# Quarter sums of two feed-forward stages moved from GpSimd to VectorE, and modulation steps placed later, in a whole diffusion-model forward pass on one core

## The chip, the core and the metric

The program runs on one core of a Trainium2 chip. A core has a matrix engine (TensorE, PE in the profile; its weight loads are PEld), three engines for elementwise work (VectorE is DVE, ScalarE is ACT, GpSimd is POOL), and SyncE (SP), whose queue issues the DMA transfers. Each engine runs its own instructions strictly in the order in which they stand, and waits at an instruction until what it needs is there. The metric is the device time of one execution, in microseconds (us); lower is better.

## The reference, cut to what matters

Two transformer-like blocks (512 tokens of `x`, 256 of `ctx`, width 1024) are computed in float32. Between attention and state-space mixers stand four gated feed-forward layers, and scales, shifts and gates come from a "modulation" product:

```python
def swiglu(h, w_in, w_out):
    gate, up = jnp.split(h @ w_in, 2, axis=-1)          # w_in 1024 x 5632, w_out 2816 x 1024
    return (jax.nn.silu(gate) * up) @ w_out
...
mod_x = jax.nn.silu(c) @ mod_w[layer] + mod_b[layer]     # six vectors of 1024; the second block has nine
mod_c = jax.nn.silu(c_ctx) @ mod_w[layer] + mod_b[layer]
shm_x, scm_x, gm_x, shf_x, scf_x, gf_x = ...
x = layer_norm(ALPHA * x + gf_x * swiglu(x * (1.0 + scf_x) + shf_x, ffn_w_in[layer], ffn_w_out[layer]), ...)
```

## The kernel before

**Float32 from two halves.** TensorE is fed with a rounded half `hi` and a remainder `lo` of every float32 operand, and three products stand for one. `split` (lines 64 and 65) makes the halves: ACT casts `whi`, then DVE subtracts to get `wlo`. Weights come in by DMA as `raw` or `sr`, 512 KB at a time.

**Two feed-forward layers in quarters.** The first and the third feed-forward layer have 768 tokens; `first_product_quarters` computes their `h @ w_in` with seven products of quarter matrices instead of eight. A step `j` (22 of them) is one block of 128 gate columns and the same 128 up columns. For `j` = 0 and 1 (`LEAD`) it works plainly, in four calls of `whole`, because the sums of the activations are not there yet; each `whole` ends in a product `lg` of ACT and DVE (lines 524 and 525) that frees its PSUM bank, and all four share one `lg` buffer. From `j` = 2 on, seven products of 12 matmuls each run per step, and their operands are sums of quarters: `h.sums` forms those of the activations once (tiles `ts`, lines 428 to 431, halved into `tq`), and `load` and `weight` form those of the weights for every `j`: four sums of 128x512 (`sx` and `sr`, line 502), 80 per layer, all on POOL. Two of the activation sums are on POOL too (lines 429 and 431, three times each). Evacuations of the step's PSUM banks are DVE's `c` (570, 579, 585) and `g` (582, 587). After the last `whole` the fourth quarter of the activations is overwritten with its sum (`fourth`, which issues casts `hhi` and subtractions `hlo`).

**Modulation between the matmuls.** Modulation vectors needed later are worked out in small steps on a list `c.fill`: for one vector there are eight `part` steps (a 512 KB load `graw` and a DVE multiply-add into `acc`, lines 228 and 230, one for `x` and often one for `ctx`), a `finish` (adds the bias, line 236, sums over partitions with matmuls of line 244, writes the row to DRAM), and a `turn` (reads the row back as `fmrow` and transposes it on PE, line 257). `c.run_fill(n)` issues the next `n` steps. In the two layers in quarters one step is run in each `whole`, after each `j` and after each group of the second product.

**The order of the work.** A scheduler places the instructions of each engine once, when the program is built; `high_priority` moves a part ahead (`WPRIO`, 400 places) or, with a negative offset, back. Weight loads, casts and sums have `WPRIO`, the multiply-adds have -150. At run time every engine keeps that order.

Of the kernel before, what the change touches and what calls it, by code (L numbers as in the profile page):

```python
# [389 lines left out]
class Quarters:  # L390
# [26 lines left out]

    def sums(self, pool):

        c, nc = self.c, self.c.nc  # L420
        rest = []
        for i in range(self.half):
            f1, f2 = (pool.tile([P, KT, P], F32, tag=f"f{j}", name=c.nm("f"), bufs=2) for j in range(2))
            nc.sync.dma_start(f1, self.fd[i])
            nc.sync.dma_start(f2, self.fd[i + self.half])
            s = pool.tile([P, 3, 4, P], F32, tag="ts", name=c.nm("ts"), bufs=1)
            s4 = pool.tile([P, 4, P], F32, tag="ts4", name=c.nm("ts4"), bufs=self.half)
            nc.vector.tensor_tensor(s[:, 0], f2[:, :4], f1[:, :4], ALU.subtract)
            nc.gpsimd.tensor_tensor(out=s[:, 2], in0=f2[:, 4:], in1=f2[:, :4], op=ALU.subtract)
            nc.vector.tensor_tensor(s[:, 1], f2[:, 4:], s[:, 0], ALU.subtract)  # L430
            nc.gpsimd.tensor_tensor(out=s4, in0=f1[:, 4:], in1=s[:, 1], op=ALU.subtract)
            o = slice(i * P, (i + 1) * P)
            c.split(s, self.t[0][:, :, :, o], self.t[1][:, :, :, o])
            rest.append((s4, o))

        def fourth():
            for s4, o in rest:
                c.split(s4, self.hi[:, 2, :, o], self.lo[:, 2, :, o])

        return fourth  # L440
# [37 lines left out]
def first_product_quarters(c, h, T, w_in, gd, nfill, pool):  # L478
# [22 lines left out]
    def sums(o, x, y, op):  # L501
        nc.gpsimd.tensor_tensor(out=o, in0=x, in1=y, op=op)

    def load(j):
        with c.tc.high_priority(offset=WPRIO):
            r = []
            for b, o in enumerate((0, FFN_H)):
                x = pool.tile([P, KT, P], F32, tag=f"sr{b}", name=c.nm("sr"), bufs=3 - b)
                nc.sync.dma_start(x, w_in[:, o + j * P : o + (j + 1) * P].rearrange("(k p) n -> p k n", p=P))
                r += [x[:, :4], x[:, 4:]]  # L510
            r.append(pool.tile([P, 4, P], F32, tag="sx", name=c.nm("sx"), bufs=2))
            raw[j] = r
            sums(r[4], r[0], r[2], ALU.subtract)
            sums(r[2], r[2], r[3], ALU.add)

    with c.tc.tile_pool(name=c.nm("fs"), bufs=1) as fp:
        ws = [[c.wcols(w_in, o + j * P) for o in (0, FFN_H)] for j in range(LEAD)]

        def whole(j, v, outs):
# [6 lines left out]
            nc.sync.dma_start(gd[j][:, v * n : v * n + n], g)  # L526
            c.run_fill(nfill)

        for j in range(LEAD):
            whole(j, 0, (one(j), two(j)))  # L530
        fourth = h.sums(fp)
        for j in range(LEAD, LEAD + 2):
            load(j)
        for j in range(LEAD):
            whole(j, 1, (c.ps("px")[:, :n], c.ps("px")[:, :n]) if j % 2 == 0 else (one(0), two(0)))
        fourth()

# [6 lines left out]
    with c.tc.tile_pool(name=c.nm("fm"), bufs=1) as mp:  # L544
        W, S, X = {}, {}, {}

        def weight(j, i, hi, lo):

            if j not in raw:
                load(j)  # L550
            r = raw[j]
            c.split(r[{1: 0, 2: 1, 3: 1, 4: 3, 5: 2, 6: 0, 7: 4}[i]], hi, lo)
            if i == 1:
                sums(r[0], r[3], r[4], ALU.subtract)
            elif i == 2:
                sums(r[1], r[1], r[0], ALU.subtract)
            W[j, i] = hi, lo

        def run(j, i):
# [23 lines left out]
            elif i == 3:  # L583
# [4 lines left out]
                nc.sync.dma_start(gd[j], g)  # L588
                c.run_fill(nfill)

        for s in range(0, len(order), 2):
            with c.tc.high_priority(offset=WPRIO):
                hi = c.whl.tile([P, 2, 4, P], F32R, tag="hi", name=c.nm("whi"))
# [582 lines left out]
def main(c, I, out, stop=None):  # L1176
# [6 lines left out]
    modp = [None]  # L1183

    def accs(pool):
        return lambda: pool.tile([P, D], F32, tag="acc", name=c.nm("acc"))
# [91 lines left out]
    with tc.tile_pool(name="mix0", bufs=1) as mp:  # L1278
        mix = mp.tile([P, 6, D], F32, name="mix")
        og, od = mix[:, :, :512], mix[:, :, 512:]  # L1280
        with tc.tile_pool(name="dif", bufs=1) as dp:
# [10 lines left out]
            with tc.tile_pool(name="gla", bufs=1) as gp:  # L1292
# [4 lines left out]
                modp[0] = lambda: df.pair()[:, :D]  # L1297
                c.fill += block1(0, 2, "gm0", "row") + block1(0, 4, "scf0", "fm") + block1(0, 3, "shf0", "fm")
                c.run_fill(3)
# [54 lines left out]
    with tc.tile_pool(name="modp1", bufs=2) as mq:  # L1354
        modp[0] = accs(mq)
        c.fill += block1(0, 5, "gf0", "row") + block1(1, 1, "scm1", "fm") + block1(1, 0, "shm1", "fm")
        c.fill += block1(1, 2, "gm1", "row", False) + block1(1, 4, "scf1", "fm", False)
        c.fill += block1(1, 3, "shf1", "fm", False)
        ln = LnTail(c, None, I, 0, 1, 6, {v: f"gf0{v}" for v in "xc"}, xdt(0),
                    ln_sc("01", 0, 1, "scm1", "shm1", "xc"), xd[1], "xc" if stop else "x", 768,  # L1360
                    out=out if stop == "ln2" else None)
        ffn(c, h, 768, I["ffn_w_in"][0], I["ffn_w_out"][0], ln, (1, 1))
        h = ln.h
# [31 lines left out]
    with tc.tile_pool(name="modp2", bufs=2) as mq:  # L1395
        modp[0] = accs(mq)
        c.fill += block1(1, 5, "gf1", "row", False) + block2(0, "fm") + block2(1, "fm") + block2(2, "row")
        ln = LnTail(c, None, I, 1, 1, 4, {"x": "gf1x"}, xdt(2), lambda: ada_sc(0, 0, "xc"), xd[3], "x", 768,
# [18 lines left out]
    with tc.tile_pool(name="modp3", bufs=2) as mq:  # L1417
        modp[0] = accs(mq)
        c.fill += block2(3, "fm") + block2(4, "fm") + block2(5, "row", False) + block2(6, "fm", False)
        c.fill += block2(7, "fm", False) + block2(8, "row", False)  # L1420
        ad = AdaTail(c, None, 6, lambda pool: ada_gate(pool, 0, 2, 0.5, "xc"),
                     lambda t: xdt(3)(t) if t < 4 else ctx2(t), lambda: ada_sc(1, 3, "xc"), xd[0], 768,
                     out if stop == "f1" else None)
        ffn(c, h, 768, I["ffn1_w_in_2"][0], I["ffn1_w_out_2"][0], ad, (1, 1))
        h = ad.h
# [744 lines left out]
```

## Time and profile before

| | |
|---|---|
| Runs without the profiler | 3641.51, 3643.37, 3630.83 us (median 3641.51) |
| Profiled execution | 3632.67 us, of which the span of the trace is 3630.9 us |
| Busy share of the span | PE 94%, PEld 80%, DVE 65%, ACT 45%, POOL 18% |
| Mean granted clock of PE | 0.974 of full speed |
| DMA | 522.53 MB, mean 144 GB/s |

The first layer in quarters begins its first product at about 543 us and ends it at about 905 us; the third layer does so from about 2110 to 2451 us. In both, POOL is busy 33 to 43% of the time.

### The profile page before, as it was taken

What the parts mean: (1) busy time and instruction counts of PE and PEld (TensorE: products, weight loads), DVE (VectorE), ACT (ScalarE), POOL (GpSimd) and SP (SyncE); (2) the same over time, 40 slices, a digit from 0 to 9 for tenths busy, and PEclk for the clock granted to TensorE, in tenths of its full rate; (3) what the DMA queues carried; (4) which work ended last, traced back from release to release, by engine and by line L of the source; (5) the groups of instructions that cost most, each with busy time, mean ns of one, the idle gap of its engine ahead of it and who ended that gap; (6) DMA issues with size and microseconds to landing.
All of it is one profiled execution on the core that took longest, in us unless ns stands there. A gap on an engine that the chain in (4) does not pass through costs nothing.

```text
span 3630.9 us, 48754 instructions
## 1 busy us (share of the span) xinstructions
PE 3412.6 (94%) x18316; PEld 2903.6 (80%) x18316; DVE 2372.8 (65%) x3578; ACT 1641.7 (45%) x2719; POOL 649.9 (18%) x481
## 2 busy tenths in 40 slices
PE   8999987999989999988999979999999999999998
PEld 5877776999778877767887769998787798878887
DVE  6766667676687577766566786766766585663235
ACT  5335533444345555533334634343556454553234
POOL 0001124433020354443000133430000000000000
PEclk9999998999999999989999989999999999999999
DMA  6330135443774333344666753436751122354356
GB/s 226 111 88 27 47 116 181 134 125 102 244 249 149 87 101 103 101 157 160 219 196 203 261 189 104 134 114 221 252 183 40 52 63 73 108 180 151 119 169 217
DMA packets 446834, 522.53 MB, mean 144 GB/s; under 512 B 21272, under 2 KB 357268, under 8 KB 446597
## 3 DMA queue, kind: packets, MB, share of 16 engines
q1 hardware_dynamic: 446597, 519.41, 45.0%
q8 instruction: 144, 2.36, 0.3%
q14 instruction: 93, 0.76, 0.1%
HBM read 452.49 MB, written 62.64 MB: 142 GB/s over the span
## 4 chain that ended last, share of the span: by engine, by line
PE 34%; issue 9%; DVE 4%; DMA 4%; ACT 2%; POOL 1%; SPq 0%; DVEq 0%; POOLq 0%; ACTq 0%
PE big L99 7%; PE big L113 5%; PE px L113 5%; PE px L496 4%; PE px L99 4%; PE big L496 3%; DMA gr<-gd 1%; DVE wlo L65 1%; PE mm L1606 1%; PE mm L1779 1%; PE big L1571 1%; ACT whi L64 1%; PE mm L1600 1%; PE big L1569 0%; DVE acc L230 0%
## 5 line engine op out<-in xcount | busy, mean ns | idle before, releaser
L65 DVE TENSOR_TENSOR wlo<-raw,whi 128x1024 fp32r<-128x1024 f32 (+1 forms) x444 | 542.3, 1226 | 476.3 <-ACT whi L64 440.9
L64 ACT CAST whi<-raw 128x1024 fp32r<-128x1024 f32 (+1 forms) x444 | 457.7, 1033 | 673.7 <-PE big L99 216.4
L99 PE MATMUL big<-hhi,whi 128*128 128x512 f32 (+1 forms) x1312 | 444.9, 364 | 10.0 <-ACT hhi L64 5.8
L99 PE MATMUL big<-hlo,whi 128*128 128x512 f32 (+1 forms) x1312 | 437.6, 359 | 5.3 <-DVE hlo L65 5.3
L99 PE MATMUL big<-hhi,wlo 128*128 128x512 f32 (+1 forms) x1312 | 439.4, 360 | 0.0
L133 POOL TENSOR_TENSOR s<-s,mhalf 128x1 f32<-128x1 f32 (+1 forms) x106 | 76.3, 721 | 1989.0 <-DVE s L131 1976.0
L99 PEld LDWEIGHTS big<-hhi,whi 128*128 128x128 f32 x1312 | 237.6, 192 | 55.1 <-issue 7.8
L99 PEld LDWEIGHTS big<-hlo,whi 128*128 128x128 f32 x1312 | 236.4, 191 | 42.9 <-DVE hlo L65 6.6
L99 PEld LDWEIGHTS big<-hhi,wlo 128*128 128x128 f32 x1312 | 236.3, 191 | 37.2 <-issue 1.9
L230 DVE SCALAR_TENSOR_TENSOR acc<-graw,silu_c,acc 128x1024 f32<-128x1024 f32 x168 | 223.9, 1355 | 33.5 <-DMA graw<-in_mod_w_dram 16.4
L65 DVE TENSOR_TENSOR wlo<-sr,whi 128x512 fp32r<-128x512 f32 x240 | 187.0, 813 | 60.6 <-ACT whi L64 59.9
L64 ACT CAST whi<-sr 128x512 fp32r<-128x512 f32 x240 | 139.3, 618 | 183.5 <-PE big L496 84.4
L113 PE MATMUL px<-whi,hhi 128*128 128x256 f32 (+1 forms) x712 | 213.2, 302 | 0.1
L113 PE MATMUL px<-wlo,hhi 128*128 128x256 f32 (+1 forms) x712 | 211.1, 299 | 0.0
L113 PE MATMUL px<-whi,hlo 128*128 128x256 f32 (+1 forms) x712 | 210.5, 299 | 0.0
L113 PE MATMUL big<-wlo,ghi 128*128 128x512 f32 x616 | 193.5, 395 | 2.4 <-DVE wlo L65 2.3
L113 PE MATMUL big<-whi,glo 128*128 128x512 f32 x616 | 192.3, 393 | 0.0
L113 PE MATMUL big<-whi,ghi 128*128 128x512 f32 x616 | 192.2, 394 | 0.0
L496 PE MATMUL px<-tq,whi 128*128 128x384 f32 x640 | 165.1, 338 | 4.8 <-DVE tq L65 2.5
L496 PE MATMUL big<-hhi,whi 128*128 128x384 f32 x416 | 143.6, 345 | 26.2 <-DVE lg L525 22.9
L64 ACT CAST ghi<-gr 128x256 fp32r<-128x256 f32 (+1 forms) x176 | 79.7, 458 | 150.0 <-DMA gr<-gd 91.6
L496 PE MATMUL big<-hhi,wlo 128*128 128x384 f32 x416 | 142.8, 344 | 1.7 <-DVE wlo L65 1.7
(594 smaller groups left out, 8265.0 us busy)
## 6 DMA issues: line engine op xcount, KB each, us to landing
raw<-in_ffn_w_out_dram SPq DMA_DIRECT2D x176, 512.0 KB
raw<-in_ffn_w_in_dram SPq DMA_DIRECT2D x96, 512.0 KB
graw<-in_mod_w_dram SPq DMA_DIRECT2D x80, 512.0 KB
sr<-in_ffn_w_in_dram SPq DMA_DIRECT2D x80, 512.0 KB
graw<-in_w_ada_dram SPq DMA_DIRECT2D x72, 512.0 KB
raw<-in_mix_w_in_dram SPq DMA_DIRECT2D x42, 512.0 KB
raw<-in_ssd_w_in_dram SPq DMA_DIRECT2D x41, 512.0 KB
gr<-gd SPq DMA_DIRECT2D x88, 192.0 KB
```

The costliest lines, as they stand in the source:

```text
L64: self.nc.scalar.copy(hi, src)
L65: self.nc.vector.tensor_tensor(lo, src, hi.bitcast(F32), ALU.subtract)
L99: self.nc.tensor.matmul(out, lhsT=w_[:, k, :], rhs=x_[:, k, t0 : t0 + tn], start=st, stop=sp)
L113: self.nc.tensor.matmul(out, lhsT=h_[:, t0 : t0 + P], rhs=w_[:, n0 : n0 + nn], start=st, stop=sp)
L133: nc.gpsimd.tensor_tensor(out=r, in0=v, in1=self.mhalf[:, :n], op=ALU.pow)
L230: nc.vector.scalar_tensor_tensor(a, raw, v[:, k : k + 1], a, ALU.mult, ALU.add)
L496: nc.tensor.matmul(out, lhsT=w_[:, k], rhs=b_[:, k], start=start and k == 0 and w_ is wh and b_ is bh, stop=stop and k == 3 and w_ is wl, ...
L1571: nc.tensor.matmul(sc[:, o : o + kn], lhsT=qs[b][r, tt], rhs=kl[kv][r, k0 : k0 + kn], start=False, stop=True)
L1600: nc.tensor.transpose(pt[:, i - i0 : i - i0 + P], p[:, i : i + P], c.ident)
L1606: nc.tensor.matmul(po[r, :], lhsT=v[:, u, kv * 64 : kv * 64 + 64], rhs=pT[:, i * P : (i + 1) * P], start=i == 0, stop=i == len(keys) - 1)
L1779: nc.tensor.matmul(pa[:, ts_], lhsT=QK[:, 1, ts_], rhs=Q[:, ts_], start=True, stop=True)
```

## The change

All sums of quarters go from POOL to DVE: lines 429 and 431 of `h.sums` and the helper `sums`. The two weight sums `sx` and `sr` are no longer issued in `load` but in `weight`, after the first split of that `j`. `fourth` is issued a few products later, its tile `ts4` lives in a pool that stays open, and the first weight tiles of the quarters get a priority offset of 50 instead of 400. `whole` runs no modulation step any more, nor do `j` = 2 and 3; in exchange each later `j` runs two (the argument `nfill` falls back to `(2, 1)`). `mods` builds the list of steps so that the last step of a vector, its `turn`, comes after five steps of the next vector.

```diff
-    def sums(self, pool):
+    def sums(self, pool, keep):
...
-            s4 = pool.tile([P, 4, P], F32, tag="ts4", name=c.nm("ts4"), bufs=self.half)
+            s4 = keep.tile([P, 4, P], F32, tag="ts4", name=c.nm("ts4"), bufs=self.half)
             nc.vector.tensor_tensor(s[:, 0], f2[:, :4], f1[:, :4], ALU.subtract)
-            nc.gpsimd.tensor_tensor(out=s[:, 2], in0=f2[:, 4:], in1=f2[:, :4], op=ALU.subtract)
             nc.vector.tensor_tensor(s[:, 1], f2[:, 4:], s[:, 0], ALU.subtract)
-            nc.gpsimd.tensor_tensor(out=s4, in0=f1[:, 4:], in1=s[:, 1], op=ALU.subtract)
+            nc.vector.tensor_tensor(s[:, 2], f2[:, 4:], f2[:, :4], ALU.subtract)
             o = slice(i * P, (i + 1) * P)
             c.split(s, self.t[0][:, :, :, o], self.t[1][:, :, :, o])
+            nc.vector.tensor_tensor(s4, f1[:, 4:], s[:, 1], ALU.subtract)
...
     def sums(o, x, y, op):
-        nc.gpsimd.tensor_tensor(out=o, in0=x, in1=y, op=op)
+        nc.vector.tensor_tensor(o, x, y, op)
...
-            r.append(pool.tile([P, 4, P], F32, tag="sx", name=c.nm("sx"), bufs=2))
-            raw[j] = r
-            sums(r[4], r[0], r[2], ALU.subtract)
-            sums(r[2], r[2], r[3], ALU.add)
+        r.append(pool.tile([P, 4, P], F32, tag="sx", name=c.nm("sx"), bufs=2))
+        raw[j] = r
...
             nc.sync.dma_start(gd[j][:, v * n : v * n + n], g)
-            c.run_fill(nfill)
...
-        fourth = h.sums(fp)
+        fourth = h.sums(fp, pool)
...
-        fourth()
...
             if i == 1:
+                sums(r[4], r[0], r[2], ALU.subtract)
+                sums(r[2], r[2], r[3], ALU.add)
                 sums(r[0], r[3], r[4], ALU.subtract)
...
-                c.run_fill(nfill)
+                if j >= LEAD + 2:
+                    c.run_fill(nfill)
 
         for s in range(0, len(order), 2):
-            with c.tc.high_priority(offset=WPRIO):
+            if s == 4:
+                fourth()
+            with c.tc.high_priority(offset=WPRIO if s > 8 else 50):
...
+    def mods(*sets):
+
+        late = None
+        for steps in sets:
+            for i, f in enumerate(steps[:-1]):
+                c.fill.append(f)
+                if i == 4 and late:
+                    c.fill.append(late)
+            late = steps[-1]
+        c.fill.append(late)
...
-        ffn(c, h, 768, I["ffn_w_in"][0], I["ffn_w_out"][0], ln, (1, 1))
+        ffn(c, h, 768, I["ffn_w_in"][0], I["ffn_w_out"][0], ln)
...
-        ffn(c, h, 768, I["ffn1_w_in_2"][0], I["ffn1_w_out_2"][0], ad, (1, 1))
+        ffn(c, h, 768, I["ffn1_w_in_2"][0], I["ffn1_w_out_2"][0], ad)
```

The list of steps is built with `mods` in all four places that filled it before (in the first mixer and in three feed-forward layers).

The order of DVE's instructions shows what the scheduler made of it. At the beginning of the first layer, ahead of the second `lg` (it frees the bank of the second `whole`), stood before:

```order
L65 TENSOR_TENSOR wlo_1105_5497<-sr_1091_5358,whi_1104_5496 128x512 x2
L230 SCALAR_TENSOR_TENSOR acc_1075_5261<-graw_1102_5482,silu_c_88,acc_1075_5261 128x1024
L65 TENSOR_TENSOR wlo_1110_5535<-sr_1094_5365,whi_1109_5534 128x512 x2
L65 TENSOR_TENSOR wlo_1115_5573<-sr_1091_5358,whi_1114_5572 128x512
L65 TENSOR_TENSOR wlo_1115_5573<-sr_1092_5360,whi_1114_5572 128x512
L525 TENSOR_TENSOR lg_1077_5314<-big_1059_5180,lg_1077_5314 128x384
```

and now, on the same engine at the same place (lines after 433 are smaller by two in this part of the new file):

```order
L65 TENSOR_TENSOR wlo_1099_5469<-sr_1087_5348,whi_1098_5468 128x512 x2
L230 SCALAR_TENSOR_TENSOR acc_1162_5952<-graw_1180_6087,silu_c_88,acc_1162_5952 128x1024
L65 TENSOR_TENSOR wlo_1104_5509<-sr_1090_5353,whi_1103_5508 128x512 x2
L502 TENSOR_TENSOR sx_1089_5352<-sr_1087_5348,sr_1088_5350 128x512
L502 TENSOR_TENSOR sr_1088_5350<-sr_1088_5350 128x512
L502 TENSOR_TENSOR sr_1087_5348<-sr_1088_5350,sx_1089_5352 128x512
L502 TENSOR_TENSOR sx_1092_5357<-sr_1090_5353,sr_1091_5355 128x512
L523 TENSOR_TENSOR lg_1074_5308<-big_1059_5180,lg_1074_5308 128x384
```

Four sums on DVE's own queue stand where two subtractions stood that waited for ACT's casts of POOL's sums. The multiply-add L230 is still there: the scheduler took the loads and multiply-adds of the steps that are now issued from `j` = 4 on and put them where the steps of `whole` were. On SP's queue the loads at this place are the same in kind and number. Counted to the first `c` of line 570, DVE then has three sums, one `wlo`, three `ts`, `lg`; five `ts`, one sum, three `wlo`, two `tq`, `lg`; four `ts`, two `hlo` and one `tq` (the third `hlo` stands behind that `c`).

At the beginning of the third layer, ahead of the last `lg` (it frees the bank of the fourth `whole`), the last ten DVE rows before were:

```order
L65 TENSOR_TENSOR wlo_3432_18592<-sr_3409_18379,whi_3431_18591 128x512
L428 TENSOR_TENSOR ts_3406_18369<-f_3405_18366,f_3404_18365 128x512
L65 TENSOR_TENSOR hlo_3121_17292<-ts4_3399_18346,hhi_3120_17291 128x4x128
L430 TENSOR_TENSOR ts_3406_18369<-f_3405_18366,ts_3406_18369 128x512
L65 TENSOR_TENSOR hlo_3121_17292<-ts4_3403_18358,hhi_3120_17291 128x4x128
L65 TENSOR_TENSOR wlo_3435_18624<-sx_3410_18381,whi_3434_18623 128x512
L65 TENSOR_TENSOR wlo_3435_18624<-sr_3411_18384,whi_3434_18623 128x512
L236 TENSOR_TENSOR acc_3392_18280<-acc_3392_18280,brow_3524_19270 1x1024
L65 TENSOR_TENSOR tq_3374_18197<-ts_3406_18369,tq_3373_18196 128x12x128
L525 TENSOR_TENSOR lg_3418_18497<-big_3375_18198,lg_3418_18497 128x384
```

and now the last twelve are:

```order
L65 TENSOR_TENSOR wlo_3421_18528<-sr_3407_18372,whi_3420_18527 128x512
L502 TENSOR_TENSOR sr_3404_18367<-sr_3404_18367 128x512
L428 TENSOR_TENSOR ts_3402_18359<-f_3401_18356,f_3400_18355 128x512
L430 TENSOR_TENSOR ts_3402_18359<-f_3401_18356 128x512
L429 TENSOR_TENSOR ts_3402_18359<-f_3401_18356,ts_3402_18359 128x512
L502 TENSOR_TENSOR sx_3409_18376<-sr_3407_18372,sr_3408_18374 128x512
L433 TENSOR_TENSOR ts4_3403_18360<-f_3400_18355,ts_3402_18359 128x512
L502 TENSOR_TENSOR sr_3408_18374<-sr_3408_18374 128x512
L65 TENSOR_TENSOR tq_3374_18197<-ts_3402_18359,tq_3373_18196 128x12x128
L502 TENSOR_TENSOR sr_3407_18372<-sr_3408_18374,sx_3409_18376 128x512
L65 TENSOR_TENSOR wlo_3421_18528<-sr_3407_18372,whi_3420_18527 128x512
L523 TENSOR_TENSOR lg_3413_18479<-big_3375_18198,lg_3413_18479 128x384
```

The three `hlo` of `fourth` and the bias row L236 have moved behind the `lg`, and sums have come ahead of it. From the third `lg` of this layer to the last one DVE now has seven sums, four `ts`, three `wlo` and two `tq`.

For the `turn` of a vector, SP's queue shows the distance between the write of its row (L248) and its reading back (L255). For vector `m7x` of the second block it was

```order
L248 DMA row_m7x_22530<-acc_3970_21974 1x1024
L224 DMA graw_4136_22665<-in_w_ada_2_dram 128x1024
L74 DMA raw_4137_22668<-in_ffn1_w_out_2_dram 128x1024
L630 DMA gr_4154_22740<-gd_3364_18183 128x384
L255 DMA fmrow_4113_22562<-row_m7x_22530 8x128
```

and is now

```order
L248 DMA row_m7x_21894<-acc_3890_21578 1x1024
L224 DMA graw_3988_22026<-in_w_ada_2_dram 128x1024
L74 DMA raw_3994_22043<-in_ffn1_w_out_2_dram 128x1024
L74 DMA raw_4000_22055<-in_ffn1_w_out_2_dram 128x1024
L631 DMA gr_4009_22073<-gd_3370_18189 128x384
L74 DMA raw_4006_22067<-in_ffn1_w_out_2_dram 128x1024
L631 DMA gr_4054_22256<-gd_3349_18168 128x384
L224 DMA graw_4050_22247<-in_w_ada_2_dram 128x1024
L74 DMA raw_4051_22250<-in_ffn1_w_out_2_dram 128x1024
L631 DMA gr_4060_22268<-gd_3350_18169 128x384
L255 DMA fmrow_4077_22368<-row_m7x_21894 8x128
```

so that ten transfers lie between them instead of four. On PE the transpose of `m7x` now stands 247 matmuls behind the last matmul of line 244 for that vector (43 before), that of `m6x` 109 (58 before), and that of `m4c` 241 (123 before).

## Rows read from the trace of the kernel before

**Rows 1.** The page: engines over the whole span, and PE's clock in 40 slices
```profile
PE 3412.6 (94%) x18316; PEld 2903.6 (80%) x18316; DVE 2372.8 (65%) x3578; ACT 1641.7 (45%) x2719; POOL 649.9 (18%) x481
PEclk9999998999999999989999989999999999999999
```

**Rows 2.** Stretches: length, busy us (instructions) by engine, PE clock, DMA share, GB/s
```profile
584.00:628.00 44.00, 24.40 (x89) 22.33 (x88) 34.35 (x30) 14.76 (x24) 25.58 (x17) 0.69 0.49 172
628.00:640.00 12.00, 12.00 (x71) 12.00 (x71) 11.31 (x14) 4.95 (x10) 2.20 (x1) 1.00 0.41 127
640.00:900.00 260.00, 251.80 (x1427) 246.72 (x1426) 183.47 (x243) 112.23 (x216) 105.81 (x68) 0.99 0.39 121
2156.00:2176.00 20.00, 8.47 (x35) 8.15 (x34) 17.24 (x17) 7.27 (x14) 9.81 (x6) 0.66 0.11 36
```

**Rows 3.** PE in order of time, the instructions after its long waits
```profile
591.67 0.69 PE L496 MATMUL big<-hhi,whi 128*128 128x384 f32 x1 [5.52 <-DVE lg L525]
610.92 0.69 PE L496 MATMUL big<-hhi,whi 128*128 128x384 f32 x1 [5.80 <-DVE lg L525]
2170.44 0.69 PE L496 MATMUL big<-hhi,whi 128*128 128x384 f32 x1 [11.53 <-DVE lg L525]
```

**Rows 4.** ACT, POOL and DVE in order of time, 574 to 623 us
```profile
583.72 1.29 POOL L502 TENSOR_TENSOR sx<-sr,sr 128x512 f32<-128x512 f32 x1 [15.46 <-DMA sr<-in_ffn_w_in_dram]
...
587.62 1.14 ACT L64 CAST whi<-sr 128x512 fp32r<-128x512 f32 x2 [6.54 <-POOL sr L502]
...
588.27 2.87 DVE L65 TENSOR_TENSOR wlo<-sr,whi 128x512 fp32r<-128x512 f32 x2 [5.63 <-ACT whi L64]
...
588.89 1.71 POOL L502 TENSOR_TENSOR sx<-sr,sr 128x512 f32<-128x512 f32 x1
...
594.43 1.76 DVE L65 TENSOR_TENSOR wlo<-sx,whi 128x512 fp32r<-128x512 f32 x1
...
603.09 0.68 DVE L430 TENSOR_TENSOR ts<-f,ts 128x512 f32<-128x512 f32 x1
...
607.45 1.29 DVE L65 TENSOR_TENSOR wlo<-sr,whi 128x512 fp32r<-128x512 f32 x2
...
619.15 1.75 DVE L65 TENSOR_TENSOR tq<-ts,tq 128x1536 fp32r<-128x1536 f32 x1
...
622.62 1.01 DVE L570 TENSOR_TENSOR c<-big,p 128x384 f32<-128x384 f32 x2
```

**Rows 5.** DVE's `lg` at the third layer's beginning, in order of time
```profile
2147.05 0.54 DVE L525 TENSOR_TENSOR lg<-px,lg 128x384 f32<-128x384 f32 x1
2169.84 0.54 DVE L525 TENSOR_TENSOR lg<-big,lg 128x384 f32<-128x384 f32 x1
```

**Rows 6.** Groups by form, DVE, 640 to 900 us: busy, mean ns, idle before
```profile
L65 DVE TENSOR_TENSOR wlo<-sr,whi 128x512 fp32r<-128x512 f32 x101 | 79.1, 815 | 20.4 <-ACT whi L64 20.2
L230 DVE SCALAR_TENSOR_TENSOR acc<-graw,silu_c,acc 128x1024 f32<-128x1024 f32 x20 | 30.2, 1522 | 0.1
L65 DVE TENSOR_TENSOR wlo<-sx,whi 128x512 fp32r<-128x512 f32 x17 | 15.9, 937 | 8.9 <-ACT whi L64 8.9
```

**Rows 7.** The same groups, 905 to 1000 us, where POOL does nothing
```profile
L230 DVE SCALAR_TENSOR_TENSOR acc<-graw,silu_c,acc 128x1024 f32<-128x1024 f32 x15 | 19.0, 1282 | 7.5 <-DMA graw<-in_mod_w_dram 7.5
...
L65 DVE TENSOR_TENSOR wlo<-sr,whi 128x512 fp32r<-128x512 f32 x2 | 1.3, 688 | 2.4 <-ACT whi L64 2.4
```

**Rows 8.** Waits of PE for `fmrow`, over the whole span
```profile
PE mm L257 <- DMA fmrow<-row_m4c: 4.0, 1, 4.0
...
PE mm L257 <- DMA fmrow<-row_m6x: 2.6, 1, 2.6
...
PE mm L257 <- DMA fmrow<-row_m7x: 2.0, 1, 2.0
```

**Rows 9.** Waits of PE between 640 and 900 us, all of them
```profile
PE big L496 <- DVE c L570: 5.8, 3, 3.5
PE big L496 <- DVE c L585: 2.4, 2, 1.4
```

More of the change, by code (lines that the diff above doesn't have):

```diff
@@ L501, in sums @@
     def sums(o, x, y, op):
-        nc.gpsimd.tensor_tensor(out=o, in0=x, in1=y, op=op)
+        nc.vector.tensor_tensor(o, x, y, op)
     def load(j):
+        r = []
         with c.tc.high_priority(offset=WPRIO):
-            r = []
             for b, o in enumerate((0, FFN_H)):
@@ L1297, in main @@
                 modp[0] = lambda: df.pair()[:, :D]
-                c.fill += block1(0, 2, "gm0", "row") + block1(0, 4, "scf0", "fm") + block1(0, 3, "shf0", "fm")
+                mods(block1(0, 2, "gm0", "row"), block1(0, 4, "scf0", "fm"), block1(0, 3, "shf0", "fm"))
                 c.run_fill(3)
@@ L1355, in main @@
         modp[0] = accs(mq)
-        c.fill += block1(0, 5, "gf0", "row") + block1(1, 1, "scm1", "fm") + block1(1, 0, "shm1", "fm")
-        c.fill += block1(1, 2, "gm1", "row", False) + block1(1, 4, "scf1", "fm", False)
-        c.fill += block1(1, 3, "shf1", "fm", False)
+        mods(block1(0, 5, "gf0", "row"), block1(1, 1, "scm1", "fm"), block1(1, 0, "shm1", "fm"),
+             block1(1, 2, "gm1", "row", False), block1(1, 4, "scf1", "fm", False), block1(1, 3, "shf1", "fm", False))
         ln = LnTail(c, None, I, 0, 1, 6, {v: f"gf0{v}" for v in "xc"}, xdt(0),
@@ L1396, in main @@
         modp[0] = accs(mq)
-        c.fill += block1(1, 5, "gf1", "row", False) + block2(0, "fm") + block2(1, "fm") + block2(2, "row")
+        mods(block1(1, 5, "gf1", "row", False), block2(0, "fm"), block2(1, "fm"), block2(2, "row"))
         ln = LnTail(c, None, I, 1, 1, 4, {"x": "gf1x"}, xdt(2), lambda: ada_sc(0, 0, "xc"), xd[3], "x", 768,
@@ L1418, in main @@
         modp[0] = accs(mq)
-        c.fill += block2(3, "fm") + block2(4, "fm") + block2(5, "row", False) + block2(6, "fm", False)
-        c.fill += block2(7, "fm", False) + block2(8, "row", False)
+        mods(block2(3, "fm"), block2(4, "fm"), block2(5, "row", False), block2(6, "fm", False),
+             block2(7, "fm", False), block2(8, "row", False))
         ad = AdaTail(c, None, 6, lambda pool: ada_gate(pool, 0, 2, 0.5, "xc"),
```

## The prediction

> **What bounds the kernel now.** I read the page first, then stretches of time, then the waits of the engine that they point to, then the single instructions around those waits. The page [rows 1] has PE busy for 94% of the span, far ahead of DVE with 65%; the time is set by PE wherever it runs without a gap, and what can be won lies in its gaps and in its clock. The line of the clock drops to 8 at slices 7, 18 and 24; slices 7 and 24 hold the beginnings of the two layers in quarters, the first and the third. The stretches [rows 2] show the size. Undisturbed, PE ran 71 matmuls in 12.0 us, 0.169 us each. From 584 to 628 us it ran 89, worth 15.0 us, at a mean clock of 0.69: 29 us of 44 were lost, to idle time and to the lower of the two clock levels (1.2 in place of 2.4 GHz). From 2156 to 2176 us it ran 35, worth 5.9 us: 14 us lost. After that, from 640 to 900 us, the clock was 0.99, and PE waited for 8.2 us in all [rows 9]: there PE is the bound and DVE has 30% to spare.
>
> Who made PE wait is in its order of time [rows 3]: 5.52 and 5.80 us in the first layer, 11.53 us in the third, each for an `lg` of DVE, which frees a PSUM bank. Those `lg` were late for a reason that begins at POOL [rows 4]. POOL's first sum started at 583.72 us, when its load had landed; ACT's cast of a later sum waited 6.54 us for POOL and began at 587.62; DVE's `wlo` waited 5.63 us for that cast; and `lg` stood behind that `wlo` on DVE. Then DVE itself became slow. A subtraction of 128x512 took 0.68 us where POOL was quiet (603.09 us), and two in a row 1.29 us, so each next one costs 0.61. While POOL was adding, the same size took 1.76 us (594.43). One POOL sum beside a DVE operation thus cost DVE some 1.1 us more than doing the sum itself would.
>
> **The change, part by part.** The sum is made against the profiled execution, 3632.67 us, of which 3630.9 are span.
>
> *Sums on DVE, beginning of the first layer.* The order of the instructions gives what DVE has to do, the rows its prices: 0.61 us for 128x512, 1.75 for `tq` [rows 4], about 0.5 for `lg` [rows 5]. The fourth load has landed at 583.72 us, and the fifth at the latest when POOL took it without a wait, at 588.89 [rows 4]. Four sums (2.4 us) and the `lg` then put the second `lg` between 586.7 and 590; I take 587, since in the trace the loads follow each other and only POOL was late. It was at 591.07, half a microsecond before PE went on [rows 3]. To the third `lg` there are now seven operations and itself, 4.8 us; to the fourth nine, two `tq` and itself, 9.5 us; to the first `c` six and one `tq`, 5.4 us. That puts the fourth `lg` at 601.3 instead of just before 610.92 [rows 3], and `c` at 606.7 instead of 622.62 [rows 4]: 16 us. DVE is not alone: ACT casts `tq` in between, each `lg` needs the single buffer that the DMA before it empties, and PE's shorter gaps may still cost it some clock. I take off 3 us: **13 us gained**, bounds 5 (if the loads arrive late and the chain through ACT stays) and 18.
>
> *The same, beginning of the third layer.* Between the third and the fourth `lg` there were 22.8 us [rows 5]. Now DVE has 14 operations of 128x512 (8.5 us), two `tq` (3.5) and the `lg` between them: 12.5 us. With the third `lg` where it was, the fourth comes at 2159.6 us, 0.7 us after PE ran out of work (2170.44 less 11.53 [rows 3]). So about 10.8 us of the wait go, and the matmuls behind it no longer run at the low level. Of the 14 us lost I keep 2: **12 us gained**, bounds 6 and 14.
>
> *Steps of modulation taken out of the beginning.* For the beginning I price this at nothing: the order shows the same loads on SP and the same multiply-adds on DVE before the same `lg`, only for steps that are issued later in the code. Had they gone, the five multiply-adds after the first `lg` of the first layer would have freed about 6 us of DVE.
>
> *The rest of the two first products.* For each `j` DVE gets four sums, and from 640 to 900 us there are 17 `j` [rows 6]: 68 times 0.61 is 41 us. It loses the contention: `wlo` took 815 and 937 ns there against 688 where POOL did nothing, the multiply-add 1522 against 1282 [rows 6, 7]. That is 101 times 0.127, 17 times 0.25 and 20 times 0.24, together 22 us. Two steps run per `j` instead of one: by the order, about 18 multiply-adds more stand in the same stretch, 23 us, and some 5 us of their last steps. 183 + 41 - 22 + 28 is 230 us of 260: DVE goes from 70 to 88%. I take **0** for PE, because weights are made ahead: in this stretch DVE's `wlo` waits for ACT and not PE for `wlo` [rows 6, 9]. The bounds are a gain of 8 us (the 8.2 us of waits [rows 9] vanish in both layers' share) and a loss of 40 us per layer, below. What is queued behind a sum on DVE is the next `wlo` and the evacuations `c` and `g`; a sum whose load is late now holds these up, where before only POOL stood still. The loads are the same 512 KB pieces, at a DMA share of 0.39 [rows 2].
>
> The Trainium skill (Perfetto Trace Analysis, Optimizing Scalar/DVE Operations) says that a saturated DVE may be relieved by giving work to GpSimd, and warns that the two share a read port, so that it might not help. By its first half the change is a mistake in this stretch: the sums would come back in full, 41 us of DVE per layer, and it is the first rival below. By its second half most comes back as faster DVE instructions; the rows above show 22 of the 41 us, so the trace lies between the two.
>
> *The `turn` steps.* PE waited 4.0, 2.6 and 2.0 us for rows that had just been written to DRAM [rows 8]. All three transposes now stand 100 to 250 matmuls behind the end of their vector, at least 18 us at 0.169, against 43 to 123 before. **8 us gained**, bounds 0 (the read is still issued on SP just ahead of the transpose) and 9.
>
> *The second products* get 24 steps instead of 36 and end without any; DVE had room there, so 0, bounds 0 and 4 us gained.
>
> Sum: 13 + 12 + 0 + 8 = 33 us, from 3632.7 to 3599.7. The profiled execution lies 8.8 us under the median of the runs, within their scatter of 12.5 us; 33 us off the median gives 3608.5. I state 3606, nearer to the median, since that is what is compared.
>
> **The rivals.**
>
> *DVE becomes the bound in the first products (slower).* Besides the 183 us busy, DVE stood still for 76 of 260 us. If all these waits stayed and 47 us of work came on top, the stretch would grow to about 306 us: 46 more, less a little, say 40 us per layer. Two layers, less the 33 us gained: 3641.5 + 80 - 33 = 3688 us. It turns slower than before from the point where more than half of the 76 us remain as waits that cannot be filled. For it: in-order DVE at 88%, with bursts of four multiply-adds. Against it: the biggest waits named, 29 us, are for ACT's casts `whi` [rows 6], and ACT was busy for only 112 of the 260 us [rows 2]; a cast can be made earlier, while DVE is late, so these waits should shrink as DVE fills.
>
> *Little comes of it.* The beginning is held by the loads and by ACT's chain rather than by the sums: DVE now stands still for a load that only POOL waited for. Then the lower bounds hold, 5 + 6 + 3 us, and some of the crowding costs a little: 3641.5 - 14 = 3627. For it: POOL's first wait was 15.46 us, for a load [rows 4]. Against: the loads had begun to land by 583.72 us, and what came after that was slow on POOL and DVE.
>
> *More comes of it.* PE's clock no longer falls at either beginning, the waits [rows 9] go too: 18 + 14 + 8 + 9 = 49 us, 3592 off the median.
>
> *That the change doesn't do what it says* is true of one part only, the steps of modulation at the beginning, and is in the sum with nothing.
>
> **How the numbers follow.** Forecast (18 to 42 us gained) 0.57, more 0.12, little 0.21, slower through DVE 0.10. The range goes from the whole of "more" taken off the profiled execution, 3632.7 - 49 = 3583 us, to half of "little" taken off the median, 3641.5 - 7 = 3634; the slower case and the poorest outcomes of "little", together about 0.2, are left out. A measurement of this kernel tells 0.5%, 18 us, from no change. Faster than that: the first two cases, 0.69. Within: "little" and a part of a mild crowding, 0.23. Slower: 0.08.
>
> **What the profile of the changed kernel would show.** POOL nearly empty in both layers; DVE's 128x512 operations at 0.6 to 0.7 us throughout; PE's waits for `lg` under 5 us each in the first layer and under 2 in the third, with a clock above 0.9 from 2156 to 2176 us; DVE at 85 to 90% in the rest of the first products with PE at 97% as now; no PE wait for `fmrow` over 1 us. I would be wrong if PE then waits for `wlo`, or for `c` and `g` by tens of microseconds, if the sums wait on DVE for `sr`, or if the clock still falls at the beginnings.

## The result and the profile after

The changed kernel takes 3587.67 us (median of four runs, 3585.56 to 3596.36) where the kernel before took 3636.17 (four runs). The ratio is 0.9871, 95% interval 0.9842 to 0.9901; measured again later it was 0.9866 (0.9849 to 0.9884). That is 48 us faster; 35 were forecast, off the median known then. The profiled execution took 3588.99 us, 43.7 less than the one before, and all comparisons of stretches below are between profiled executions.

The page of the changed kernel, engines over the span and PE's clock in 40 slices, stands against [rows 1]:

```profile
PE 3398.8 (95%) x18316; PEld 2890.5 (81%) x18316; DVE 2388.1 (67%) x3750; ACT 1641.4 (46%) x2719; POOL 378.7 (11%) x309
PEclk9999999999999999989999989999999999999999
```

DVE has taken over 172 instructions and is busy for only 15 us more, while POOL is busy for 271 us less. The stretches, to be read against [rows 2] (length, busy us and instructions of PE, PEld, DVE, ACT, POOL, then clock, DMA share, GB/s); the third layer now runs some 10 us earlier, so its two stretches are taken 10 us earlier than before:

```profile
584.00:628.00 44.00, 33.51 (x168) 31.77 (x167) 39.34 (x59) 19.43 (x33) 0.00 (x0) 0.88 0.62 201
640.00:900.00 260.00, 258.48 (x1480) 253.35 (x1479) 216.96 (x333) 117.88 (x224) 0.00 (x0) 1.00 0.47 145
2146.00:2166.00 20.00, 19.94 (x116) 19.62 (x115) 19.39 (x30) 10.58 (x22) 0.00 (x0) 1.00 0.29 83
2170.00:2430.00 260.00, 260.00 (x1492) 255.97 (x1491) 205.84 (x325) 119.35 (x228) 0.00 (x0) 1.00 0.44 142
```

Counted in matmuls at the undisturbed 0.169 us, the beginning of the first layer got 168 done instead of 89 (13.4 us gained), that of the third 116 instead of 35 (13.7 us). In the rest of the first products 1480 instead of 1427 ran in the first layer (9.0 us gained). In the third PE did not stand still for one microsecond; in the kernel before, 2180 to 2440 us, it ran 1406 in the same 260 us:

```profile
2180.00:2440.00 260.00, 249.74 (x1406) 244.39 (x1405) 178.32 (x232) 110.14 (x212) 101.21 (x68) 0.99 0.38 119
```

That is 86 matmuls, 14.5 us. The first products as a whole agree. From the start of the first matmul of line 496 to the start of the last one, the kernel before took 380.4 us in the first layer (543.42 to 923.83) and 382.1 in the third (2098.47 to 2480.60), so there they begin and end otherwise than the 2110, 905 and 2451 us given with the times before. The changed kernel took 359.5 and 355.1 us: 20.9 and 27.0 us less, where the windows give 22.4 and 28.2.

PE's waits over 0.5 us from 575 to 630 us, against the first two of [rows 3] (from 2130 to 2180 us PE now has no wait over 0.2 us):

```profile
589.80 0.44 PE L496 MATMUL big<-hhi,whi 128*128 128x384 f32 x1 [0.82 <-DVE lg L523]
592.29 0.44 PE L496 MATMUL px<-hhi,whi 128*128 128x384 f32 x1 [1.16 <-ACT lg L522]
604.87 0.69 PE L496 MATMUL big<-hhi,whi 128*128 128x384 f32 x1 [7.00 <-DVE lg L523]
610.96 0.45 PE L496 MATMUL px<-tq,whi 128*128 128x384 f32 x1 [1.16 <-DVE tq L65]
```

And DVE in order of time at the same place, to be read against [rows 4]: sums, `lg` and the first `c`, with every 128x512 operation at 0.68 us:

```profile
588.52 0.68 DVE L502 TENSOR_TENSOR sx<-sr,sr 128x512 f32<-128x512 f32 x1
589.19 0.56 DVE L523 TENSOR_TENSOR lg<-big,lg 128x384 f32<-128x384 f32 x1
...
593.88 0.55 DVE L523 TENSOR_TENSOR lg<-px,lg 128x384 f32<-128x384 f32 x1
...
604.25 0.56 DVE L523 TENSOR_TENSOR lg<-big,lg 128x384 f32<-128x384 f32 x1 [1.08 <-ACT lg L522]
...
610.82 1.01 DVE L568 TENSOR_TENSOR c<-big,p 128x384 f32<-128x384 f32 x2
```

The wait that is left, 7.00 us, is no longer for a sum. ACT's own half of that `lg` stood still until the DMA before had emptied the single `lg` buffer (ACT in order of time):

```profile
603.73 0.49 ACT L522 ACTIVATE lg<-big 128x384 f32<-128x384 f32 x1 [2.53 <-DMA gd<-lg]
```

DVE's groups from 640 to 900 us, to be read against [rows 6, 7], show where its time went and came from:

```profile
L65 DVE TENSOR_TENSOR wlo<-sr,whi 128x512 fp32r<-128x512 f32 x99 | 64.4, 684 | 8.6 <-ACT whi L64 8.6
L230 DVE SCALAR_TENSOR_TENSOR acc<-graw,silu_c,acc 128x1024 f32<-128x1024 f32 x36 | 45.5, 1276 | 1.4 <-DMA graw<-in_mod_w_dram 1.3
L502 DVE TENSOR_TENSOR sr<-sr 128x512 f32<-128x512 f32 x32 | 21.8, 681 | 0.1
...
L585 DVE TENSOR_TENSOR g<-c,c 128x384 f32<-128x384 f32 x17 | 9.4, 550 | 0.1
```

All of PE's waits in that stretch, against [rows 9], are now

```profile
PE big L113 <- DVE c L583: 0.9, 1, 0.9
PE big L496 <- DVE c L568: 0.6, 1, 0.6
```

One stage became slower. From the last matmuls of line 293 that wait for `y` to the last ones of line 275 that wait for `xr`, around the second feed-forward layer, the kernel before took 405.5 us (1724.05 to 2129.57). The changed one took 415.5, by these two rows of PE in order of time:

```profile
1704.07 1.94 PE L293 MATMUL mm<-cfs,y 128*128 128x128 f32 x8 [3.27 <-ACT y L984]
...
2119.58 1.97 PE L275 MATMUL mm<-cfs,xr 128*128 128x128 f32 x8 [5.62 <-ACT xr L1173]
```

### The profile page after: what moved, and what is told of

The parts are those of the page before. It is cut to its first block, busy times and chain, and to the rows that moved or that the text cites. A ratio compares the mean times of both kernels' runs of the same rounds, so it can differ in the third digit from the quotient of the medians.

```text
span 3587.2 us, 48491 instructions
## 1 busy us (share of the span) xinstructions
PE 3398.8 (95%) x18316; PEld 2890.5 (81%) x18316; DVE 2388.1 (67%) x3750; ACT 1641.4 (46%) x2719; POOL 378.7 (11%) x309
## 4 chain that ended last, share of the span: by engine, by line
PE 39%; DMA 6%; DVE 4%; ACT 3%; issue 2%; POOL 0%; SPq 0%; DVEq 0%; POOLq 0%; ACTq 0%
PE big L99 11%; PE big L113 6%; PE px L496 5%; PE px L99 4%; PE px L113 4%; PE big L496 4%; DMA raw<-in_ffn_w_out_dram 2%; DVE wlo L65 1%; PE mm L1617 1%; DMA gr<-gd 1%; PE mm L1790 1%; DMA raw<-in_ffn_w_in_dram 1%; ACT whi L64 1%; DMA graw<-in_w_ada_dram 1%; PE big L1582 1%
## 5 line engine op out<-in xcount | busy, mean ns | idle before, releaser
L230 DVE SCALAR_TENSOR_TENSOR acc<-graw,silu_c,acc 128x1024 f32<-128x1024 f32 x168 | 214.0, 1290 | 29.7 <-DMA graw<-in_w_ada_dram 19.6
L65 DVE TENSOR_TENSOR wlo<-sr,whi 128x512 fp32r<-128x512 f32 x240 | 156.2, 684 | 22.5 <-ACT whi L64 22.5
L65 DVE TENSOR_TENSOR glo<-gr,ghi 128x256 fp32r<-128x256 f32 (+1 forms) x176 | 92.8, 530 | 90.3 <-ACT ghi L64 82.3
```

The source lines that it names most:

```text
L65: self.nc.vector.tensor_tensor(lo, src, hi.bitcast(F32), ALU.subtract)
L230: nc.vector.scalar_tensor_tensor(a, raw, v[:, k : k + 1], a, ALU.mult, ALU.add)
```

## The experiments

**The parts of the change, each alone on the kernel before.** Sums of quarters on DVE:

```diff
-        nc.gpsimd.tensor_tensor(out=o, in0=x, in1=y, op=op)
+        nc.vector.tensor_tensor(o, x, y, op)
...
             if i == 1:
+                sums(r[4], r[0], r[2], ALU.subtract)
+                sums(r[2], r[2], r[3], ALU.add)
```

(and the two of `h.sums`, lines 429 and 431, with their order in `h.sums`; `sx` and `sr` leave `load` for `weight`.) Expected:

> The kernel before, with nothing changed but the quarter sums: on DVE, and those of the input weights issued where the first of them is used. If the sums carry the change (less contention, no chain through POOL): both beginnings gain what the changed kernel gained there, 15 and 14 us, and PE's waits for c and g in the rest of the first products go as well, 10 us or more; about 3636 - 40 = 3596 us. If the changed kernel's gain came from the steps of modulation that no longer stand at the beginnings, or from the later place of the fourth sums: less than 15 us gained, 3621 or more. If DVE becomes the bound with the steps still at the beginnings: slower than before.

Measured: 3595.06 us, ratio 0.9861 (0.9846 to 0.9876), the same as the whole change. From 640 to 900 us it ran 1486 matmuls, and DVE was busy for 197 us. Its two first products took 358.1 and 357.0 us.

```profile
584.00:628.00 44.00, 33.62 (x159) 31.98 (x159) 41.99 (x59) 19.22 (x33) 0.00 (x0) 0.84 0.63 205
640.00:900.00 260.00, 258.91 (x1486) 255.44 (x1485) 197.47 (x315) 115.22 (x219) 0.00 (x0) 1.00 0.40 123
```

The steps of modulation:

```diff
             nc.sync.dma_start(gd[j][:, v * n : v * n + n], g)
-            c.run_fill(nfill)
...
-                c.run_fill(nfill)
+                if j >= LEAD + 2:
+                    c.run_fill(nfill)
...
-        ffn(..., (1, 1))
+        ffn(...)
```

> The kernel before, with only the steps of modulation moved: none in the first products' beginning, two per j from the fifth j on, as in the changed kernel; the sums stay on POOL. The order says that the scheduler pulls later steps forward, so that DVE has the same multiply-adds at the beginning. If that holds: within 8 us of before, and PE's waits for lg at the third layer's beginning still near 11 us. If the steps did crowd the beginning: 10 to 20 us faster, with the fourth lg of the first layer some 6 us earlier after the second.

Measured: 3656.84 us, ratio 1.0036 (1.0023 to 1.0048), slower. PE's waits for `lg` were as before, 10.9 us from 570 to 640 us and 11.5 at the third layer's beginning: the beginning was not relieved. The rest was worse: from 640 to 900 us PE waited 8.5 us for `c` of line 569 alone, 28 multiply-adds instead of 20 stood there at 1575 ns each, and DVE was busy for 195 us. The two first products took 394.5 and 385.5 us. I had expected no effect beyond 8 us; the cost of two steps per `j` on a DVE that is slowed by POOL was missing.

The last step of each vector, moved back by `mods` in all four places:

> The kernel before, with only the last step of each vector issued five steps later. My theory: the 4.0, 2.6 and 2.0 us of PE's waits for fmrow go, and in the layer between the two in quarters something is lost, as in the changed kernel (weights land late there at two places, 4.5 us of waits, and PE ran some 10 us longer from 1724 to 2090 us): together between 6 us faster and 4 us slower. Rival: what was lost in that layer has nothing to do with these steps; then 8 us faster.

Measured: 3652.32 us, ratio 1.0025 (1.0016 to 1.0035): slower by 9 us by the ratio, outside both expectations. The stage around the second feed-forward layer took 419.7 us instead of 405.5, and PE waited there for weights, which it did not in this stage of the kernel before (PE's waits, 1690 to 1980 us):

```profile
PE big L99 <- ACT whi L64: 6.4, 3, 3.5
...
PE big L99 <- DVE wlo L65: 2.5, 3, 1.1
```

**The changed kernel with one part undone.** With the sums of the weights on POOL (the one line of the helper; the six of `h.sums` stay on DVE):

> The changed kernel with every quarter sum on POOL again, all else kept. If the sums carry the change: most of the gain goes, 3620 to 3640 us, PE waits 10 us and more for lg at the beginnings again, and DVE's wlo takes 0.8 us and more. If the place of the steps and of the fourth sums carries it: 3590 to 3605.

Measured: 3643.86 us, ratio 1.0004 (0.9991 to 1.0017). The whole gain is gone, and the first products take 383.5 and 381.1 us. But it is not lost where it was made:

```profile
584.00:628.00 44.00, 32.89 (x160) 31.11 (x159) 39.27 (x44) 19.07 (x32) 22.59 (x12) 0.84 0.57 187
640.00:900.00 260.00, 246.77 (x1374) 239.35 (x1373) 196.55 (x248) 111.28 (x216) 99.45 (x65) 0.98 0.41 125
```

The beginning of the first layer has 160 matmuls, as many as with the sums alone on DVE (159), although POOL adds there for 22.6 us. So this beginning is relieved with the weight sums on POOL too, as long as the rest of the change stays: the six sums of the activations on DVE, the weight sums issued in `weight`, `fourth` and the first weights placed later. Which of these does it was not tried alone. At the third layer's beginning PE waited 6.4 us for `lg`, about half of the 11.5 before. The loss lies in the rest, 1374 matmuls against 1427 before, with two steps per `j` beside POOL, as in the kernel with the steps alone.

With the steps of modulation in the first products as before:

> The changed kernel with the steps of modulation in the first products as before: one per block from the beginning on, 12 at the beginning instead of none. If what it cost in the kernel before (0.36%, 13 us) was two steps per j on a DVE beside POOL's sums, and DVE has room now: no cost, and with the sums on DVE the beginning is no longer short of DVE either, so within 8 us of the changed kernel, 3588. If two steps per j cost the same with the sums on DVE: 3575.

Measured: 3605.36 us, ratio 0.9900 (0.9885 to 0.9916), where the changed kernel has 0.9871 and 0.9866. So this part, which cost 0.36% with the sums on POOL, seems to gain about 0.3% with the sums on DVE (the intervals are apart for the second measurement of the changed kernel, not for the first); I had expected nothing or the opposite. With `fourth` and the priority as before:

> The changed kernel with the fourth sums at their old place, made right after the beginning from a pool of their own, and with the old priority of the first weights. If the place matters: the fourth lg of the first layer and the first c come some microseconds later, and both layers lose, 3592 to 3600. If DVE has them in the same order anyhow: 3588.

Measured: 3596.78 us, ratio 0.9883 (0.9866 to 0.9900): on the side of a loss, but the intervals overlap. In its profile PE waited 4.18 and 5.19 us for the two `lg` of the first layer where the changed kernel's waited 0.82 and 7.00. With the last steps in their old order, everywhere or beside the second feed-forward layer alone:

```diff
-        mods(block1(1, 5, "gf1", "row", False), block2(0, "fm"), block2(1, "fm"), block2(2, "row"))
+        c.fill += block1(1, 5, "gf1", "row", False) + block2(0, "fm") + block2(1, "fm") + block2(2, "row")
```

> The changed kernel with the last step of each vector back in its old place everywhere. If the whole move costs what it cost in the kernel before (0.25%, 9 us): 3578. My prediction's theory, that it saves 8 us by the waits for fmrow: 3596, and waits of PE for fmrow are back.

> The changed kernel, with the steps of the second modulation stage (gf1 and m0 to m2, beside the layer between the two in quarters) in their old order. If the moved last steps cost time in that layer, by weights that are issued later on SP: PE's two pairs of waits for whi and wlo near 1790 and 1851 us go, about 10 us faster than the changed kernel, 3577. If they do not, and what was lost in that layer is the clock of one execution: 3587.

Measured: everywhere 3585.44 us, ratio 0.9854 (0.9833 to 0.9876); beside the second layer alone 3582.87, ratio 0.9843 (0.9825 to 0.9862). With the old order everywhere PE's waits for `fmrow` came back, 4.6 us for `m7x` and 4.5 for `scf1x`, and yet the time cannot be told from that of the changed kernel: it lies between the two expectations and decides for neither. The other version was run again next to the changed kernel on one chip:

> The changed kernel again, on the same chip as the next one: 0.987 of the kernel before, as at first.

> The changed kernel with the second modulation stage's steps in their old order, again, for its difference to the changed kernel on one chip: 5 to 10 us faster, if the waits for whi and wlo in the layer between are the cause; the same, if the first measurement (0.9843 against 0.9871) was scatter.

Measured: 3587.94 and 3580.49 us, ratios 0.9866 (0.9849 to 0.9884) and 0.9843 (0.9824 to 0.9862). The intervals still overlap, so the 7 us are likely and not certain; it has the best median of all kernels run. What is plain is the stage. Its length was 404.9 and 407.4 us in the two profiles of this version, 406.7 with no step moved, 405.5 and 407.4 in the kernel before and in the one with only the sums on DVE; in the seven profiles, the changed kernel's among them, in which these steps were moved back and both ends of the stage have a row, it was 412.9 to 419.7. The rows of SP's queue say how. In the changed kernel (SP in order of time):

```profile
1778.80 0.24 SPq L248 DMA_DIRECT2D row_gf1x<-acc  x1
1782.19 0.32 SPq L456 DMA_DIRECT2D gd<-g  x1
1782.55 0.43 SPq L174 DMA_DIRECT2D gatex<-row_gf1x  x1
1783.08 1.47 SPq L74 DMA_DIRECT2D raw<-in_ffn_w_in_dram  x2
```

and with the old order (run next to it):

```profile
1773.66 0.23 SPq L248 DMA_DIRECT2D row_gf1x<-acc  x1
1774.00 0.38 SPq L74 DMA_DIRECT2D raw<-in_ffn_w_in_dram  x1
1774.88 0.33 SPq L174 DMA_DIRECT2D gatex<-row_gf1x  x1
```

A weight load `raw` that went out 0.34 us after the row now stands behind the store `gd<-g`, which waits for DVE, and behind the reading of the row; it goes out 4.28 us after the row. ACT then stands still for a load, and PE behind it for `whi` and `wlo` (ACT and PE of the changed kernel in order of time):

```profile
1789.48 1.04 ACT L64 CAST whi<-raw 128x1024 fp32r<-128x1024 f32 x1 [10.71 <-DMA raw<-in_ffn_w_in_dram]
```

```profile
1790.58 0.50 PE L99 MATMUL big<-hhi,whi 128*128 128x512 f32 x1 [1.55 <-ACT whi L64]
1791.83 0.50 PE L99 MATMUL big<-hhi,wlo 128*128 128x512 f32 x1 [0.53 <-DVE wlo L65]
```

Waits of PE for `whi` and `wlo` make 7.0 of the 10 us in this stage of the changed kernel (1720 to 2090 us), and none are left in the version with the old order; the rows show one of the places. SP's waits for `g` (line 456, 1690 to 1960 us) were 32.0 us in the changed kernel and 18.1 in this one.

**POOL beside DVE, and DVE's room.** Two kernels add one useless addition for each quarter sum of the weights, on POOL or on DVE; nothing but the reuse of the buffer waits for it:

```diff
+    def extra(x):
+        d = pool.tile([P, 4, P], mybir.dt.bfloat16, tag="dm", name=c.nm("dm"), bufs=1)
+        nc.gpsimd.tensor_tensor(out=d, in0=x, in1=x, op=ALU.add)
...
                 sums(r[4], r[0], r[2], ALU.subtract)
+                extra(r[3])
```

> The changed kernel, with POOL made to add once for each of the input weights' quarter sums on DVE: r[3] and itself into a tile that nothing reads (128x512, written as bfloat16, since there is no room for float32). No step of the kernel waits for it but the load that reuses the buffer of r[3]. If POOL beside DVE is what slows DVE (contention), apart from any chain: wlo back to 0.8 us and the multiply-add to 1.5 between 640 and 900 us, DVE 20 to 30 us busier there, some waits of PE for c and g again, 3600 to 3620 us. If only the chain through POOL cost time: DVE's operations at 0.68, and 3588.

> The changed kernel with the same extra additions on DVE: 64 or so between 640 and 900 us at 0.61 us, 40 us on top of 217 of 260. By the rival of my prediction (waits that stay when work is added), DVE is the bound from here on and each first product grows by most of the 40 us: 3640 to 3670. By my theory (DVE's waits are for room and shrink as it fills), DVE goes to 95% or more and PE loses little: 3595 to 3620.

Measured: on POOL 3667.32 us, ratio 1.0090 (1.0072 to 1.0108), 79 us slower than the changed kernel; on DVE 3629.88, ratio 0.9982 (0.9970 to 0.9994), 42 us slower. The same addition costs nearly twice as much on the engine that nobody waits for, and its 3667 us lie far above the 3600 to 3620 expected. The reuse of the buffer is not the reason: from 640 to 900 us SP's loads of `sr` waited for `wlo` and never for POOL. From 640 to 900 us, first with it on POOL (the stretch, then DVE's groups, then PE's longest waits):

```profile
640.00:900.00 260.00, 233.28 (x1282) 225.28 (x1281) 238.32 (x299) 101.64 (x197) 93.37 (x62) 0.97 0.40 125
```

```profile
L65 DVE TENSOR_TENSOR wlo<-sr,whi 128x512 fp32r<-128x512 f32 x92 | 68.3, 774 | 3.4 <-ACT whi L64 3.3
L230 DVE SCALAR_TENSOR_TENSOR acc<-graw,silu_c,acc 128x1024 f32<-128x1024 f32 x33 | 47.0, 1434 | 0.0
L502 DVE TENSOR_TENSOR sr<-sr 128x512 f32<-128x512 f32 x30 | 28.4, 946 | 0.0
L593 DVE TENSOR_TENSOR g<-c,c 128x384 f32<-128x384 f32 x16 | 16.3, 1017 | 0.0
```

```profile
PE big L496 <- DVE c L576: 24.3, 12, 4.3
```

then with it on DVE:

```profile
640.00:900.00 260.00, 249.45 (x1398) 239.71 (x1397) 245.98 (x388) 113.37 (x216) 0.00 (x0) 0.99 0.43 131
```

With POOL adding, the stretch holds 1282 / 1480 = 0.87 of the changed kernel's work, for which DVE would have been busy 188 us; it was busy 238. Fifty us for 62 additions is 0.81 us of DVE for each addition that it does not do itself. Counted by kinds of instruction, each against what it lasts in the changed kernel, it is some 44 us, 0.7 each. With the additions on DVE, 0.94 of the work would have taken 205 us and took 246: 41 us for 64, 0.64 each. An addition on POOL thus costs DVE at least about as much time as doing it there. The difference to PE is larger: with POOL adding it waited 24.3 us for `c` of line 576, and with the additions on DVE it had no wait for `c` over 1.2 us. Why that is so was not followed further.

## Why the prediction was right, and where its sizes were off

**The mechanism held, with one open place.** The sums alone carry the gain, and one line that takes the weight sums of the changed kernel back to POOL takes all of it. Contention is shown by itself: an addition on POOL that no step reads slows `wlo`, the multiply-add and `g` from 684, 1276 and 550 ns to 774, 1434 and 1017. One reading of its price was too high: the prediction set the 1.1 us that one subtraction lost (1.76 against 0.68) above the whole cost of a sum, though its own sum did not rest on that. Over the execution DVE does 172 instructions more, some 105 us at 0.61, and is busy for 15 us longer, so a sum on POOL had cost it about 0.5 us on average, a little less than doing it. The open place is the beginning of the first layer, which was relieved with the weight sums on POOL too.

The Trainium skill (Perfetto Trace Analysis, Optimizing Scalar/DVE Operations) warns that GpSimd and DVE share a read port, so that offloading between them might not help. By that sentence the extra additions on POOL should cost DVE something, and the trace agrees, with the three times above. The same section's advice that a saturated DVE may give work to GpSimd would lose time here: with DVE busy for 95% of the stretch, the additions cost 42 us on DVE and 79 on POOL.

**Beginning of the first layer: 13 us forecast, 13.4 measured.** The second, third and fourth `lg` were put at 587, 591.8 and 601.3 us and stood at 589.19, 593.88 and 604.25; `c` at 606.7 and 610.82. The layer itself began 2.7 us later in this execution (546.14 against 543.42), so that all four come within 1.5 us of the forecast. What I took off for the single `lg` buffer was needed: it holds the fourth `lg`, and a wait of 7.00 us is left where I had said under 5. The clock still falls behind this wait, to 0.65 to 0.69 from 600 to 615 us, which was named as a sign of being wrong. That 13 and 13.4 agree so well is luck in part: in the second profile of the changed kernel this stretch has 189 matmuls, 16.9 us gained.

**Beginning of the third: 12 forecast, 13.7 measured.** The fourth `lg` came at 2149.25, which is 2159.3 on the clock of the execution before, by the 10.1 us that the layer started earlier (2088.39 against 2098.47); 2159.6 was forecast. PE did not wait, and its clock was 1.00.

**The steps taken out of the beginning: priced at nothing there, and right.** The waits for `lg` did not change when only they were moved. What they do elsewhere was not foreseen: a loss on the kernel before, a gain on the changed one.

**The rest of the first products: 0 forecast, 19.5 us measured, and this is the term that was mis-sized.** It is 9.0 in the first layer and 14.5 in the third, less the 4.0 of `m4c` that belongs to the `turn` steps. My step said that PE gains nothing because weights are made ahead. But PE waited for `c` and `g`, and these are DVE's too; they came late because the operations ahead of them were slow, and they are on time now. I had kept this as a bound of 8 us and looked only at the first layer; the third had a wait of 3.1 us for `g` and 3.2 for `c`, and more of PE's time went with its clock, 0.99 before and 1.00 now. DVE was put at 230 of 260 us and was busy for 217 (83%), with PE at 99%: the 22 us that I counted for contention were `wlo` and the multiply-adds alone, and `g<-c,c`, another 8 us, had been left out.

**The `turn` steps: 8 forecast, about -1 measured.** The three waits of [rows 8], 8.6 us, are gone; the longest wait for `fmrow` is now 0.6 us. But the stage around the second feed-forward layer lost 10.0 us. I had followed SP's queue where the rows are read back in the quarter layers, not where the same move pushes weight loads behind a store.

13.4 + 13.7 + 19.5 + 8.6 - 10.0 is 45.2, and the profiled executions differ by 43.7. By the first and last matmuls of line 496 these 43.7 us are 20.9 and 27.0 in the two first products and 6.6 behind the last one, less 2.7 ahead of the first and 8.1 between them.

**The rivals.** DVE did not become the bound, but it was not far: 41 us more in this stretch cost 42 us over both layers, outside what either theory expected. Doubled sums are some 98 us of DVE in the two layers (80 each at 0.61), so a little over half of it was taken up by waits that shrank. "More comes of it" was nearest: the 48.5 us between the medians lie above the 18 to 42 of the main forecast and at the end of "more", which had a chance of 0.12, and the stated range held because it reached that far. They came through another sum than that of "more": more from the rest of the first products, nothing from the `turn` steps.

**Open.** Why the steps of modulation cost 0.36% on one base and gain 0.3% on the other is settled only by half: with POOL running, two steps per `j` make DVE late for `c`. Where the changed kernel wins by them was not traced to one wait. It is not in the first products, which took 356.8 and 355.4 us with the steps as before; behind the last of them that kernel took 1158 us to its end, the changed one 1144 and 1146 in its two profiles, and a part of this is the clock shown at the end.

## What to carry to other kernels

Before leaving elementwise work on GpSimd because VectorE is busy, compare the same VectorE operation with and without GpSimd running beside it, for every kind of operation in the stretch: here a 128x512 sum on GpSimd cost VectorE 0.5 us in the kernel before and 0.7 to 0.8 as an extra addition, and doing it cost 0.6. A step that is moved to remove one wait must be followed on every queue and in every stage where the helper is used; the loss here was a weight load behind a store in a stage that the change was not about. And measure the parts of a change one by one: here the whole gave 1.3%, and of the three parts tried alone one gave 1.4% and two lost.

## What the runs showed of the hardware

POOL does not slow all of DVE's operations. Where one operand lies in PSUM, 128x384 took as long beside POOL's additions as without them, while `g<-c,c`, with both operands in SBUF, went from 550 to 1017 ns. This row is of the kernel with the extra additions on POOL, 640 to 900 us:

```profile
L591 DVE TENSOR_TENSOR c<-big,u 128x384 f32<-128x384 f32 x16 | 8.8, 550 | 6.3 <-PE big L496 6.3
```

Its mean is not of instructions that missed POOL. By the times of the records, 8 of these 16 overlapped an addition of POOL and took 548 ns, the other 8 took 552. Of `g<-c,c`, 11 overlapped one and took 1231 ns, 5 did not and took 547; `wlo<-sr,whi` took 1224 ns with (16) and 679 without.

PE's clock can differ between executions where PE's waits hardly do. From 2740 to 2800 us PE was busy for 59.97 us in two kernels whose code there the change does not touch: with the steps of the first products as before

```profile
2740.00:2800.00 60.00, 59.97 (x345) 48.01 (x344) 36.30 (x91) 31.12 (x62) 1.29 (x1) 0.89 0.14 38
```

and in the changed kernel

```profile
2740.00:2800.00 60.00, 59.97 (x375) 46.94 (x374) 38.91 (x106) 31.74 (x74) 1.28 (x1) 1.00 0.13 36
```

The two windows lie some 10 to 15 us apart in the program, but the first holds thirty matmuls less at a clock of 0.89: from 2740 to 2755 us it was at 0.50 to 0.57, at or near the lower level. In both kernels PE had waited 1.3 us for ACT's `wp` (line 1594) shortly before; the clock fell behind that wait in one and stayed at 1.00 in the other. Single profiles therefore place a gain of some microseconds only where a wait goes with it; the totals above rest on the timed runs.
